# Attention's second stage: other places for biases, q and k, dense sums ahead of a step on DVE, and the last high and low parts in tiles of q and k

## The chip, the cores and the metric

The kernel runs on one core of one Trainium2 chip. A core has five engines that work beside each other, each through its own instructions in order: PE (TensorE, matmuls; the profile shows its weight loads apart, as PEld), DVE (VectorE), ACT (ScalarE), POOL (GpSimd) and SP (SyncE, which here only issues transfers). Matmuls read SBUF, the core's working memory, and write PSUM, 8 banks of 128 x 512 float32. DVE and ACT take the results from there. Transfers (DMAs) to and from DRAM are issued by SP and POOL.

The metric is the device time of one execution in microseconds (us). The profile is of one further execution, with its own time; its times are counted from the start of its span.

## What is computed

A trunk of two layers on x of 1024 tokens and 1024 features, each layer with a residual: first a gated short convolution, then dilated attention. Cut to the second layer, which the change touches:

```python
proj = rms_norm(x, attn_norm) @ w_in              # q, k, v of 3 groups, gate z
for g, (window, dilation) in enumerate(((128, 1), (512, 4), (2048, 16))):
    q, k = rms_norm(q_g, q_gain[g]), rms_norm(k_g, k_gain[g])
    logits = q @ k.T / 8 + bias_g                 # causal, banded, 16 heads of 64
    lse = logsumexp(logits)
    out_g = exp(logits - lse) @ v_g
alpha = softmax(stack(lse), axis=0)               # over the three groups
y = sum(alpha * out) * silu(z)
x = x + y @ w_out
```

All of it is float32. Large products are made of three matmuls on float32r parts: a value is split in a high part and a low part (value minus high), and high x high, high x low and low x high are added.

## The kernel before

**First stage, up to about 1649 us.** The convolution layer and the projections of q, k, v and z. Big products run as Strassen products of half size (`strassen`, `product`, L304 to L307): the right operands stand in SBUF blocks named a to g and xb, 16 KB per partition each, the weights pass through tiles `wr`, `ws` and `sr`. Normalized q and k, v and the gates go to DRAM (`qkd`, `vd`, `zd`). The last pair of products is of z. Its products read block e, then f, then, with those left over from the pair before, a, xb, d, b, g, and at the end a and b. The last value of z goes from PSUM through DVE (L316), POOL (L689) and ACT (L690, Silu) to DRAM.

**Second stage, from L812 on.** Attention on what was stored, and the output projection. All five engines run in an order written out by hand: the order in which the Python code issues instructions is the order on each engine. Heads go in 8 pairs, each with 3 groups, 24 units in all. `attention` returns for each unit 4 steps (groups 0 and 1) or 2 steps (group 2), 80 in all. A step has three parts:

- A (L887, L895, L898): PE makes the scores of q and k in two banks `ps` (a ring of 3), DVE adds the bias `bt` and takes the minimum, writing `xs`, ACT takes the exponential.
- B (L905, L843 or L845), 2 steps later (`LB`): PE transposes `xs` into `pt`, ACT or DVE copies it to `pts`.
- C (L918 or L924), 4 steps later (`LC`): PE multiplies with V into `po`; L935 copies it to `o`.

At the end of each head pair the weights of the three groups (L955 to L973) go through DRAM (`fd`) and come back spread over a tile `fb` (L981, issued by POOL). DVE scales the outputs with them (L984), POOL adds (L987), DVE multiplies with the gate (L990), and the result is split into a high part (L994, ACT) and a low part (L997, DVE) in a tile `y2`. For the last head pair there is no detour by DRAM: `wide`, `spread_last` and `last` (L1006 to L1032) do the same in halves, with tiles of the ring `qk` and PE transposes.

**The output projection** runs between the steps. The weights of a row come by `fetch` (L56), and `split` (L1075) and `split_low` (L1078) put their parts in tiles of the same ring `y2`, made by `parts_tile`, with 7 places for 16 tiles. From step 34 on, `some` issues for a step one partial sum over two head pairs (`dense`, L1064 to L1066, six matmuls) into a PSUM bank `pd`, of which there is one. `add_sums` (L1102, DVE) adds it to `acc`, in which the residual lies. There are 16 such sums for each of three rounds: steps 34 to 49, 54 to 69, and 74 to the end, where from step 80 on two come in a step, in other banks too. The fourth round, for the last two head pairs, stands at the end with its own adds (L1153) and the stores of the result.

**The loop that sets the order** goes over steps k. For each it issues, in this order of lags, A of step k, then `add_sums`, then what is due of earlier steps, C, and last B; then the dense matmuls of this step, then loads:

```python
for lag in (0, 1, LC, 3, *range(LC + 1, 15), LB):
    for f in steps[k - lag].get(lag, ()) if 0 <= k - lag < len(steps) else ():
        f()
    if lag == 0:
        add_sums()
for f in extra.get(k, ()):
    f()
```

**Memory.** Each pool's tiles get addresses in the order in which a tag is first used; pools opened later lie above. The pool `wp` (`y2`, `wraw`) lies lowest, where the first stage has its weight tiles, then `fbp` (`fb`), then `ap` (`acc`, `bt`, `qk`, `xs`, `V`, `pts`, `sz`, `o`). With `reuse_waits="tile"` a tile waits only for the last users of those earlier tiles whose memory it takes. SP's first issues of the stage are, in this order: two `bt` (L858) and two `qk` (L827) of the first unit, the same of the second, then V of the first (L835), then `bt` and `qk` of the third.

Of the kernel before, what the change touches and what calls it, by code (L numbers as in the profile page):

```python
# [10 lines left out]
F32 = mybir.dt.float32  # L11
F32R = mybir.dt.float32r
I32 = mybir.dt.int32
AF = mybir.ActivationFunctionType
OP = mybir.AluOpType
# [4 lines left out]
P = 128  # L20
D = 1024
S = 1024
KT = D // P
# [5 lines left out]
HP = H // 2  # L29
# [6 lines left out]
def trunk(ctx: ExitStack, tc: tile.TileContext, a, out):  # L36
    nc = tc.nc
# [16 lines left out]
    def raw_row(src):  # L54
        raw = wp.tile([P, 1024], F32, name="wraw", tag="wraw", bufs=2)
        nc.sync.dma_start(raw, src)  # L56
        return raw

    def parts_tile():

        t = wp.tile([P, 2, S], F32R, name="y2", tag="y2", bufs=7)
        return t

    def rsqrt(pool, src, n, name, y=None):
        if y is None:
# [64 lines left out]
    def half(hf):  # L130
        return slice(hf * HALF, hf * HALF + HALF)
# [8 lines left out]
    with tc.tile_pool(name="wq", bufs=1) as wq, tc.tile_pool(name="sle", bufs=1) as sle, \  # L140
# [197 lines left out]
        with tc.tile_pool(name="rp", bufs=1, side="right") as rp, tc.tile_pool(name="cp", bufs=2, side="right") as cp, \  # L338
# [31 lines left out]
            W = {}  # L370
# [443 lines left out]
    wp = ctx.enter_context(tc.tile_pool(name="wp", bufs=4, reuse_waits="tile"))  # L814
    with tc.tile_pool(name="sp", bufs=3, space=PSUM) as sp, tc.tile_pool(name="ptp", bufs=2, space=PSUM) as ptp, \
# [3 lines left out]
            tc.tile_pool(name="sm", bufs=2, reuse_waits="tile") as sm, \  # L819
            tc.manual_schedule(engines={getattr(mybir.EngineType, e)  # L820
                                        for e in ("PE", "DVE", "Activation", "Pool", "SP")}):
        QK, VS, SZ, y2, part = {}, {}, {}, {}, {}

        def loads(hp, g):
            QK[hp, g] = [ap.tile([P, S], F32, name="qk", tag="qk", bufs=6) for _ in range(2)]
            for i in range(2):
                nc.sync.dma_start(QK[hp, g][i], qkd[hp, g, i])  # L827
            if g == 2:
                SZ[hp] = ap.tile([P, S], F32, name="sz", tag="sz", bufs=2)
                nc.sync.dma_start(SZ[hp], zd[hp])  # L830
# [16 lines left out]
        def attention(hp, g):  # L847

            u = {}
            lo, up = slice(0, 64), slice(64, 128)  # L850
# [141 lines left out]
            def high():  # L992
                y2[hp] = parts_tile()
                nc.scalar.activation(y2[hp][:, 0], SZ[hp], AF.Copy)  # L994
# [24 lines left out]
            def last(hf, i):  # L1019
                h, z = half(hf), SZ[hp][:, half(hf)]  # L1020
                if i == 0:
                    for w in (2, 1, 0):
                        nc.vector.tensor_tensor(O[hp, w][:, h], O[hp, w][:, h], u["fb", w], op=OP.mult)  # L1023
                elif i == 1:
                    for w in (2, 0):
                        nc.vector.tensor_tensor(O[hp, 1][:, h], O[hp, 1][:, h], O[hp, w][:, h], op=OP.add)
                    nc.vector.tensor_tensor(z, O[hp, 1][:, h], z, op=OP.mult)
                    if hf == 0:
                        y2[hp] = parts_tile()
                    nc.scalar.activation(y2[hp][:, 0, h], z, AF.Copy)  # L1030
                else:
                    nc.vector.tensor_tensor(y2[hp][:, 1, h], z, y2[hp][:, 0, h].bitcast(F32), op=OP.subtract)  # L1032

            steps = []
            for q in range(2):
# [6 lines left out]
            if g == 2:  # L1042
                if hp == HP - 1:
                    todo = [(LB, weights), (3, shares), (3, wide), (LC, lambda: spread_last(0)),
                            (LC, lambda: last(0, 0)), (LC, lambda: last(0, 1))]
                    ending.update(spread=spread_last, last=last)
                else:
                    todo = [(3, weights), (LC, shares), (LC, store_shares), (LC, lambda: spread(2)),
                            (LC, lambda: spread(1)), (8, lambda: scale(2)), (8, lambda: spread(0)),
                            (9, lambda: scale(1)), (9, lambda: add(2)), (11, lambda: scale(0)),  # L1050
                            (11, lambda: add(0)), (12, gate), (13, high), (14, low)]
                for lag, f in todo:
                    end.setdefault(lag, []).append(f)
# [4 lines left out]
        W, ending = {}, {}  # L1058

        def dense(ps, kts, dt, hf, first, last):  # L1060
            ws, cs = slice(dt * P, dt * P + P), half(hf)
            for kt in kts:
                (whi, wlo), (hi, lo) = ((t[kt][:, 0], t[kt][:, 1]) for t in (W, y2))
                nc.tensor.matmul(ps, whi[:, ws], hi[:, cs], start=first and kt == kts[0], stop=False)  # L1064
                nc.tensor.matmul(ps, whi[:, ws], lo[:, cs], start=False, stop=False)  # L1065
                nc.tensor.matmul(ps, wlo[:, ws], hi[:, cs], start=False, stop=last and kt == kts[-1])  # L1066
# [6 lines left out]
        def split(kt):  # L1073
            W[kt] = parts_tile()
            nc.scalar.activation(W[kt][:, 0], raws[kt], AF.Copy)  # L1075

        def split_low(kt):
            nc.vector.tensor_tensor(W[kt][:, 1], raws[kt], W[kt][:, 0].bitcast(F32), op=OP.subtract)  # L1078

        acc = [ap.tile([P, S], F32, name="acc", tag=f"acc{dt}", bufs=1) for dt in range(KT)]  # L1080

        def residual(dt, hf):
            nc.sync.dma_start(acc[dt][:, half(hf)], x1d[dt, :, half(hf)])
# [9 lines left out]
        def some(kts, dt, hf, name):  # L1093

            ps = bank(name)
            dense(ps, kts, dt, hf, True, True)
            sums.append((ps, acc[dt][:, half(hf)]))

        def add_sums():
            while sums:  # L1100
                ps, x = sums.pop(0)
                nc.vector.tensor_tensor(x, ps, x, op=OP.add)  # L1102
# [18 lines left out]
        for r in range(3):  # L1121
            k0 = at[2 * r + 2, 0][0] + LD
            k = k0
            for i, (dt, hf) in enumerate(tiles):
                late = k >= len(steps)
                name = "pd" if not late else ("pd", ("ps", "ps", "pt", "pt")[min(k - len(steps), 3)])[i % 2]
# [9 lines left out]
            f()  # L1136
        k = 0
        while k < len(steps) + LC or any(x >= k for x in extra):
            for lag in (0, 1, LC, 3, *range(LC + 1, 15), LB):
                for f in steps[k - lag].get(lag, ()) if 0 <= k - lag < len(steps) else ():  # L1140
                    f()
                if lag == 0:
                    add_sums()
            for f in extra.get(k, ()):
                f()
            for f in begins.get(k, ()):
                f()
            k += 1
# [10 lines left out]
        for dt, hf, ps in first:  # L1159
            dense(ps, (6,), dt, hf, True, False)  # L1160
# [3 lines left out]
        for dt, hf, ps in first:  # L1164
            dense(ps, (7,), dt, hf, False, True)
# [77 lines left out]
```

## Time and profile before

| what | value |
|---|---|
| time, 3 runs | 2037.06, 2038.78, 2042.22 us; median 2038.78 |
| the profiled execution | 2040.09 us, span 2038.1 us |
| mean granted clock of TensorE | 0.988 |
| first and last score matmul (L887) | 1656.1 and 1978.0 us |
| first and last dense matmul into `pd` | 1772.8 and 2029.4 us |
| score reductions (L895) | 384, 291 ns median |
| sums (L1102) | 48, 685 ns median for those from `pd` |
| high parts of the last pair (L1030) | 2, at 2007.9 and 2017.9 us |

A row of the timeline reads: start in us, length, engine, line, operation, tile written <- tiles read, size, how many were merged; in brackets the idle time of that engine ahead of it and what ended that. A row of the waits reads: engine, what waited <- what it waited for: us in total, times, longest. A row by stretches has the stretch, its length, busy us and number of instructions of PE, PEld, DVE, ACT and POOL, the granted clock, the busy share of the DMA engines and GB/s.

### The profile page before, as it was taken

Reading aid. Unit: us, or ns where it says so; the run is one execution under the profiler, and the core shown is the slowest. Engines: PE = TensorE matmul, PEld = TensorE weight load, DVE = VectorE, ACT = ScalarE, POOL = GpSimd, SP = SyncE. Lnnn points to the kernel's source line nnn. Section 1 sums busy time; section 2 is a strip of 40 time slices with the busy share of each in tenths; the row PEclk is TensorE's granted clock in tenths of the full one; section 3 lists DMA queues with packets and bytes.
Section 4 is the critical chain, followed back from the end, with each engine's and each line's share of the span. In section 5 each row is a group of like instructions: output and inputs, shape, how many; then the busy total and the mean of one; then the engine's idle time right before and its main releaser. Section 6 shows DMA issues by size and latency. Waiting matters only on the chain. (4 is left out here: it accounts for less than half of the span.)

```text
span 2038.1 us, 29437 instructions
## 1 busy us (share of the span) xinstructions
PE 1958.5 (96%) x10302; PEld 1585.0 (78%) x10302; DVE 1481.0 (73%) x2751; ACT 903.5 (44%) x2042; POOL 879.8 (43%) x800
## 2 busy tenths in 40 slices
PE   7999999999999999999999999999999988898998
PEld 6887778888888888788888888888888866666666
DVE  6866566566666555798888888788888847767686
ACT  5433233333334344434344343444343358757570
POOL 0356566666665212434455445544445522322220
PEclk9999999999999999999999999999999999999999
DMA  5316512112214564423333233323233368766632
GB/s 189 114 62 146 141 61 73 68 67 73 72 64 152 178 228 159 131 76 111 102 105 123 84 111 97 123 83 121 86 124 104 91 241 248 219 175 207 181 115 84
DMA packets 116805, 254.25 MB, mean 125 GB/s; under 512 B 15822, under 2 KB 22718, under 8 KB 116656
## 3 DMA queue, kind: packets, MB, share of 16 engines
q1 hardware_dynamic: 93024, 177.42, 26.2%
q0 software_dynamic: 23632, 74.95, 12.9%
q8 instruction: 81, 1.33, 0.3%
q14 instruction: 68, 0.56, 0.1%
HBM read 193.05 MB, written 67.64 MB: 128 GB/s over the span
## 5 line engine op out<-in xcount | busy, mean ns | idle before, releaser
L170 DVE TENSOR_TENSOR ws<-wr,ws 128x512 fp32r<-128x512 f32 x284 | 270.2, 953 | 131.8 <-ACT ws L169 130.3
L169 ACT ACTIVATE ws<-wr 128x512 fp32r<-128x512 f32 x284 | 178.4, 630 | 395.6 <-PE pp L307 230.7
L169 ACT ACTIVATE ws<-sr 128x512 fp32r<-128x512 f32 x272 | 169.6, 629 | 295.9 <-PE pp L307 246.6
L279 POOL TENSOR_TENSOR sr<-wr 128x512 f32<-128x512 f32 x136 | 185.2, 1362 | 262.8 <-DMA wr<-in_conv_w_in 66.5
L170 DVE TENSOR_TENSOR ws<-sr,ws 128x512 fp32r<-128x512 f32 x272 | 235.6, 873 | 82.6 <-ACT ws L169 80.9
L898 ACT ACTIVATE xs<-xs,nl 128x128 f32<-128x128 f32 (+1 forms) x384 | 167.9, 439 | 91.2 <-DVE nl L895 80.2
L316 DVE TENSOR_TENSOR f<-pp,f 128x512 f32<-128x512 f32 x204 | 139.5, 684 | 85.5 <-PE pp L307 80.9
L895 DVE CUSTOM_DVE_ANT_0 xs<-ps,bt 128x128 f32<-128x128 f32 (+1 forms) x384 | 110.9, 347 | 79.5 <-PE ps L887 57.8
L312 ACT ACTIVATE f<-pp 128x512 f32<-128x512 f32 x228 | 132.5, 581 | 28.4 <-POOL blkc L683 13.4
L279 POOL TENSOR_TENSOR sr<-wr,sr 128x512 f32<-128x512 f32 x68 | 89.1, 1310 | 81.2 <-issue 57.6
L716 POOL DMA_DIRECT2D qkd<-blkc x96 | 68.1, 716 | 129.2 <-DVE blkc L711 121.8
L674 ACT ACTIVATE f<-f 128x512 f32<-128x512 f32 x96 | 60.7, 633 | 135.8 <-DVE f L316 98.8
L304 PE MATMUL pp<-blke,ws 128*128 128x512 f32 x272 | 108.7, 400 | 8.2 <-ACT f L312 8.2
L304 PE MATMUL pp<-blkg,ws 128*128 128x512 f32 x272 | 107.5, 395 | 4.8 <-ACT f L312 3.8
L306 PE MATMUL pp<-blkg,ws 128*128 128x512 f32 x272 | 106.7, 392 | 3.3 <-DVE blkg L524 3.3
L304 PE MATMUL pp<-blkf,ws 128*128 128x512 f32 x272 | 108.5, 399 | 0.7 <-ACT f L312 0.7
L304 PE MATMUL pp<-blka,ws 128*128 128x512 f32 x272 | 107.3, 395 | 0.7 <-ACT f L312 0.7
L306 PE MATMUL pp<-blke,ws 128*128 128x512 f32 x272 | 107.9, 397 | 0.0
L307 PE MATMUL pp<-blke,ws 128*128 128x512 f32 x272 | 107.8, 396 | 0.0
L304 PE MATMUL pp<-blkb,ws 128*128 128x512 f32 x272 | 107.4, 395 | 0.0
L304 PE MATMUL pp<-blkd,ws 128*128 128x512 f32 x272 | 107.0, 393 | 0.0
L887 PE MATMUL ps<-qk 64*128 64x128 f32 (+1 forms) x768 | 91.4, 355 | 15.7 <-DVE nl L895 8.6
(305 smaller groups left out, 5398.4 us busy)
## 6 DMA issues: line engine op xcount, KB each, us to landing
wr<-in_conv_w_in SPq DMA_DIRECT2D x128, 256.0 KB, 2.9
wr<-in_wqk SPq DMA_DIRECT2D x96, 256.0 KB, 3.0
qkd<-blkc POOLq DMA_DIRECT2D x96, 256.0 KB, 3.2
qk<-qkd SPq DMA_DIRECT2D x48, 512.0 KB, 7.1
wr<-in_conv_w_out SPq DMA_DIRECT2D x64, 256.0 KB, 3.2
f<-in_x SPq DMA_DIRECT2D x48, 256.0 KB, 4.5
wr<-in_wv SPq DMA_DIRECT2D x48, 256.0 KB, 2.9
vd<-f POOLq DMA_DIRECT2D x48, 256.0 KB, 2.4
```

The lines of the kernel that those rows point to most:

```text
L169: nc.scalar.activation(t[:, 0], src, AF.Copy)
L170: nc.vector.tensor_tensor(t[:, 1], src, t[:, 0].bitcast(F32), op=OP.subtract)
L279: nc.gpsimd.tensor_tensor(t, x, y, op=op)
L304: nc.tensor.matmul(ps, w[:, 0, ws], b[:, k, 0], start=new and k == 0, stop=False, skip_group_check=not new)
L306: nc.tensor.matmul(ps, w[:, 0, ws], b[:, k, 1], start=False, stop=False, skip_group_check=not new)
L307: nc.tensor.matmul(ps, w[:, 1, ws], b[:, k, 0], start=False, stop=end and k == 3, skip_group_check=not new)
L312: nc.scalar.activation(t, ps, AF.Copy)
L316: nc.vector.tensor_tensor(m, ps, m, op=OP.add)
L716: nc.gpsimd.dma_start(qkd[hp, g, which].rearrange("p (c s) -> p c s", c=c) [:, :, hf * m:(hf + 1) * m], o.rearrange("p (c s) -> p c s", c=c))
L887: nc.tensor.matmul(out_, q[hs, b * P:(b + 1) * P], k[hs, kv], start=True, stop=True)
L895: nc.vector.tensor_tensor_reduce(out=x, in0=ps[s][:, x0:x0 + nk].rearrange("p a b -> p (a b)"), in1=u["bt"][s][:, bs], op0=OP.add, op1=OP. ...
L898: nc.scalar.activation(x, x, AF.Exp, bias=nm, scale=-1.0, accum_out=L)
```

## The change

`parts_tile` moves into the second stage and takes its tiles from the pool `ap`. The tag `y2` is then first used after all others of that pool, so its 56 KB lie above them and no longer below `fb`, `acc`, `bt` and `qk`. The line of `acc` moves up within the stage; it is the pool's first tile as before. The last head pair's high and low parts are two tiles of the ring `qk` in place of one `y2` tile, and `dense` picks them by the head pair. `add_sums` is called at the head of a step, ahead of A.

```diff
-    def parts_tile():
-
-        t = wp.tile([P, 2, S], F32R, name="y2", tag="y2", bufs=7)
-        return t
...
+        def parts_tile():
+
+            t = ap.tile([P, 2, S], F32R, name="y2", tag="y2", bufs=7)
+            return t
+
         QK, VS, SZ, y2, part = {}, {}, {}, {}, {}
+        acc = [ap.tile([P, S], F32, name="acc", tag=f"acc{dt}", bufs=1) for dt in range(KT)]
...
                     if hf == 0:
-                        y2[hp] = parts_tile()
-                    nc.scalar.activation(y2[hp][:, 0, h], z, AF.Copy)
+                        y2[hp] = [ap.tile([P, S], F32R, name="qk", tag="qk", bufs=6) for _ in range(2)]
+                    nc.scalar.activation(y2[hp][0][:, h], z, AF.Copy)
                 else:
-                    nc.vector.tensor_tensor(y2[hp][:, 1, h], z, y2[hp][:, 0, h].bitcast(F32), op=OP.subtract)
+                    nc.vector.tensor_tensor(y2[hp][1][:, h], z, y2[hp][0][:, h].bitcast(F32), op=OP.subtract)
...
-                (whi, wlo), (hi, lo) = ((t[kt][:, 0], t[kt][:, 1]) for t in (W, y2))
+                whi, wlo = W[kt][:, 0], W[kt][:, 1]
+                hi, lo = y2[kt] if kt == HP - 1 else (y2[kt][:, 0], y2[kt][:, 1])
...
-        acc = [ap.tile([P, S], F32, name="acc", tag=f"acc{dt}", bufs=1) for dt in range(KT)]
...
         while k < len(steps) + LC or any(x >= k for x in extra):
+            add_sums()
             for lag in (0, 1, LC, 3, *range(LC + 1, 15), LB):
                 for f in steps[k - lag].get(lag, ()) if 0 <= k - lag < len(steps) else ():
                     f()
-                if lag == 0:
-                    add_sums()
```

## The prediction, made before the changed kernel was run

> **What bounds the kernel now.** The first view is the page's busy times, the second the busy times of each engine by stretches of the run.
>
> ```profile
> PE 1958.5 (96%) x10302; PEld 1585.0 (78%) x10302; DVE 1481.0 (73%) x2751; ACT 903.5 (44%) x2042; POOL 879.8 (43%) x800
> ...
> 1600.00:1649.00 49.00, 47.89 (x218) 38.95 (x216) 31.30 (x48) 14.89 (x26) 27.48 (x30) 1.00 0.37 113
> 1649.00:1656.00 7.00, 0.00 (x0) 0.00 (x0) 0.67 (x1) 1.91 (x2) 1.83 (x2) 0.80 0.88 280
> 1656.00:1772.00 116.00, 103.49 (x1081) 79.09 (x1081) 82.96 (x393) 96.84 (x375) 26.40 (x30) 0.92 0.81 254
> 1772.00:1990.00 218.00, 197.66 (x1804) 147.04 (x1805) 158.56 (x614) 143.12 (x535) 58.54 (x65) 1.00 0.58 170
> ```
>
> TensorE bounds the whole run. Everything before 1649 is untouched by the change. From there the columns (PE, PEld, DVE, ACT, POOL, clock, DMA) show two losses: 7.00 us with no matmul at all between the stages, and a stretch of 218.00 us, the one with the output projection's matmuls among the attention's, in which PE works 197.66 and no other engine is full. The waits name what ends them (engine waiting, line, releaser: us, times, longest):
>
> ```profile
> PE ps L887 <- DMA qk<-qkd: 7.1, 1, 7.1
> ...
> PEld pd L1064 <- DVE acc L1102: 25.6, 30, 1.2
> PE pd L1064 <- DVE acc L1102: 18.4, 26, 1.0
> ```
>
> The last two rows are of 1770 to 1990 and the same waits seen twice. I take PEld's 25.6: a weight load starts the group, and the matmul's modelled end reaches some 0.25 us into the idle time that PE's own row counts.
>
> **Part 1, tiles moved in memory.** In the order of first use, the pools lie from the end of the constants upwards. The first stage has there, by its tile sizes: wr 0 to 8 KB, ws to 40, sr to 46, block f 46 to 62, e 62 to 78, a 78 to 94, b 94 to 110, g to 126, d to 142, c to 158. Now y2 (7 x 8 KB) comes first, then wraw to 64, fb to 72, acc to 104, bt 104 to 110, q and k 110 to 134: bt lies on block b, the last block that a matmul reads. Without y2 in that pool, everything slides down by 56 KB: bt 48 to 54 on f, q and k 54 to 78 on f and e, V from 90 on a and b. acc is the first tile of its pool in both kernels, so moving its line does nothing. The change of stage, in order of time (start, length, engine, line, out<-in, idle time and releaser):
>
> ```profile
> 1626.54 0.39 PE L307 MATMUL pp<-blkf,ws 128*128 128x512 f32 x1
> ...
> 1645.83 0.39 PE L307 MATMUL pp<-blka,ws 128*128 128x512 f32 x1
> ...
> 1648.55 0.39 PE L307 MATMUL pp<-blkb,ws 128*128 128x512 f32 x1
> 1648.97 0.83 SPq L858 DMA_DIRECT2D bt<-sk  x2
> 1648.98 0.69 DVE L316 TENSOR_TENSOR f<-pp,f 128x512 f32<-128x512 f32 x1 [2.03 <-PE pp L307]
> 1649.75 1.26 POOL L689 TENSOR_TENSOR f<-f,sqacc 128x512 f32<-128x512 f32 x1 [1.30 <-DVE f L316]
> 1649.90 0.85 SPq L827 DMA_DIRECT2D qk<-qkd  x2
> 1651.04 0.63 ACT L690 ACTIVATE f<-f 128x512 f32<-128x512 f32 x1 [3.43 <-POOL f L689]
> 1651.69 1.28 ACT L898 ACT_TABLE_LOAD   x1
> 1656.08 4.31 PE L887 MATMUL ps<-qk 64*128 64x128 f32 x18 [7.15 <-DMA qk<-qkd]
> 1658.18 0.40 ACT L898 ACTIVATE xs<-xs,nl 128x128 f32<-128x128 f32 x1 [5.21 <-DVE nl L895]
> ```
>
> SP issues bt 0.03 us after the last matmul on b ends (1648.55 + 0.39); behind it wait q and k. Blocks e and f are read for the last time at 1626.54 + 0.39 = 1626.9, so the four bt and four q/k loads of the first two units can leave 22 us earlier, and 6.2 us (1649.90 to 1656.08) bring the first of them in. PE's first matmul of the stage then has its data at 1649. SP's next load, V, waits for block a until 1646.2; behind it stand bt, q, k and z of the third unit, which left at 1654 and later before, so nothing on SP becomes later. Those early loads run beside weights that are already in, in a stretch with a DMA share of 0.37: they cost nothing.
>
> What is late next is ACT, not PE. The last gate value goes DVE L316, POOL L689, ACT L690, and only then does ACT load its table, up to 1651.69 + 1.28 = 1652.97. None of these four depends on the moved tiles. Before, the first exponential started at 1658.18. From there ACT is the stage's first bound (96.84 of 116.00 us above, and nearly without a gap at first). So the gain is 1658.18 - 1652.97 = **5.2 us**, not the 7.15 of the wait. Bounds: 0 if the loads stay where they are; 10.3 if PE sets the start, since then 18 matmuls also take 1.2 us (16 take 1.16 at full clock, in the row of 1743.73 below) in place of 4.31.
>
> **Part 2, dense sums first.** A step on PE is: scores (L887), values (L924), transposes (L905), dense (L1064 to L1066) into the one bank pd. DVE's step is four to eight score reductions (L895) and only then the sum (L1102) that frees pd. Two steps, one without and one with the wait:
>
> ```profile
> 1774.43 0.71 PE L887 MATMUL ps<-qk 64*128 64x128 f32 x8
> ...
> 1778.53 1.13 PE L887 MATMUL ps<-qk 64*128 64x256 f32 x8
> ...
> 1783.19 0.40 PE L1066 MATMUL pd<-y,y 128*128 128x512 f32 x1
> 1783.51 1.14 PE L887 MATMUL ps<-qk 64*128 64x256 f32 x8
> 1784.79 0.43 DVE L895 CUSTOM_DVE_ANT_0 xs<-ps,bt 128x256 f32<-128x256 f32 x1 [2.59 <-PE ps L887]
> 1786.17 0.68 DVE L1102 TENSOR_TENSOR acc<-pd,acc 128x512 f32<-128x512 f32 x1
> 1786.91 0.19 PEld L1064 LDWEIGHTS pd<-y,y 128*128 128x128 f32 x1 [0.88 <-DVE acc L1102]
> 1788.50 0.72 PE L887 MATMUL ps<-qk 64*128 64x128 f32 x8
> ```
>
> The first step takes 1778.53 - 1774.43 = 4.10 us, the second 1788.50 - 1783.51 = 4.99; the difference is the wait of 0.88. The sum's operand is complete at 1783.19 + 0.40 = 1783.6, and DVE sits idle for 2.59 us until 1784.79 for the scores. Put at the head, the sum runs there, 1783.6 to 1784.3: it ends before the reductions can start, delays nothing on DVE or ACT, and frees pd at 1784.3, when PE wants it at 1786.91 - 0.88 = 1786.0. It adds no instruction and no new wait, for the scores come later on PE than the dense sums that it waits for. So the 25.6 us go, except where DVE is late itself:
>
> ```profile
> 1819.24 1.22 DVE L997 TENSOR_TENSOR y<-sz,y 128x1024 fp32r<-128x1024 f32 x1
> ...
> 1821.95 0.19 PEld L1064 LDWEIGHTS pd<-y,y 128*128 128x128 f32 x1 [0.93 <-DVE acc L1102]
> ```
>
> Here DVE is free at 1820.46, the sum would end at 1821.1, PE wants the bank at 1821.0: 0.1 to 0.5 stays, at three such places 1 us. Shorter steps leave DVE 158.56 and ACT 143.12 us in some 192: no bound. I take off 0.5 more for single waits behind them: **24.1 us**. Bounds: 12 if half of the waits return in another place, 26.8 with 0.6 us more at the two places where stretches without dense work, bound by DVE, begin one sum earlier.
>
> **Part 3, the last high and low parts in q/k tiles.** They no longer wait for a y2 tile that the dense matmuls still read:
>
> ```profile
> ACT y L1030 <- PE pt L1066: 12.0, 1, 12.0
> ...
> 2012.56 1.71 PE L1016 MATMUL ps<-ident,qk 64*128 64x64 f32 x24
> 2013.30 1.88 DVE L1023 TENSOR_TENSOR o<-o,ps 128x512 f32<-128x512 f32 x3 [3.79 <-PE ps L1016]
> 2015.10 0.68 DVE L1032 TENSOR_TENSOR y<-sz,y 128x512 fp32r<-128x512 f32 x1
> 2015.84 0.51 PE L1065 MATMUL pt<-y,y 128*128 128x512 f32 x1 [1.15 <-DVE y L1032]
> ```
>
> ACT's 12.0 us vanish, but nobody waits for it: L1032 stands on DVE behind three multiplications that PE's transposes release at 2013.30, and PE's 1.15 us hang on that. The tiles (4th and 5th of the ring of six behind the three that L1006 and L1008 fill) were last read by score matmuls some 20 us earlier. Worth 0; its cover is that DVE order. In the last steps no scores are left, so the moved sums stand where they stood.
>
> **The sum.** 5.2 + 24.1 + 0 = 29.3 us. The profiled execution took 2040.09 us (span 2038.1 and 2.0 around it), so it becomes 2010.8; against the median of 2038.78 that is **2009.5 us**.
>
> **Rivals.** (a) The scale factors come late. They go by DRAM (store, then four loads of fb), and their time does not shrink with the steps:
>
> ```profile
> 1710.77 1.22 DVE L984 TENSOR_TENSOR o<-o,fb 128x1024 f32<-128x1024 f32 x1 [3.96 <-DMA fb<-fd]
> 1712.89 2.07 PE L887 MATMUL ps<-qk 64*128 64x128 f32 x14 [3.56 <-DVE nl L895]
> ...
> 1743.73 1.16 PE L887 MATMUL ps<-qk 64*128 64x128 f32 x16
> ...
> 1776.28 2.09 POOL L981 DMA_DIRECT2D fb<-fd  x4 [2.54 <-DMA fd<-fo]
> 1787.37 1.22 DVE L984 TENSOR_TENSOR o<-o,fb 128x1024 f32<-128x1024 f32 x1
> fb<-fd POOLq DMA_DIRECT2D x4, 256.0 KB, 9.8
> ```
>
> L984 needs the first two of the four, which leave at 1776.28 and 1776.80 and at 9.8 us, the median of the four, land by 1786.6. It starts at 1787.37, and would come up two removed waits of 0.88 and one sum of 0.68 earlier, at 1784.9. So a wait of up to 1.7 us is possible; at 2 us in each of five head pairs that is 10 us, and 2019.5. (b) **The slower side** is the same mechanism as it stands at 1710: a wait of 3.96 us on DVE holds back the scores, PE stands for 3.56 and then runs 14 matmuls in 2.07 where 16 take 1.16 (about 3 us until it is back at full pace). At 6.5 us in five head pairs that is 33 against the 29.3 won: 2042. It decides from some 3.5 us of lateness on; for it speaks that the stretch up to 1772 has it twice, against it that the stretch from 1772 has no row of it and a DMA share of 0.58, not 0.81. (c) The loads do not move, because something else holds SP: gain 24.1, 2014.7. Against it: SP's rows show nothing of its own between the last weight and bt. (d) PE, not ACT, sets the start: 10.3 + 24.1, 2004.4. The profile's row gives the price of a cold start, 18 matmuls in 4.31 us after 7.15 of idleness. [...]
>
> **How the numbers follow.** Forecast (2006 to 2013): 0.65. (a) 0.15, (c) 0.06, (d) 0.08, (b) 0.03, no change because both waits turn into others 0.03. A measurement here tells changes above 0.3% (6 us) from none. Only (b) ends slower, only the last within 6 us: faster 0.94, same 0.03, slower 0.03. The range runs from (d) with the upper bound of part 2 (10.3 + 26.8 = 37.1, so 2002) to (a) at 2020.
>
> **What would show it.** Part 1: bt issued near 1627, PE's pause at 1649 gone, the first exponential close to 1653; if the table load comes later, the 5.2 shrink. Part 2: the row PEld pd from DVE acc falls from 25.6 to about 1, steps of 4.1 us; if waits of pd remain with DVE busy, or fb appears among the releasers of L984 after 1770, (a) is at work. Part 3: L1030 waits no more, and PE's 1.15 us at the end stay. A pause of PE above 3 us anywhere after 1656 would make the forecast wrong.

## The result, and the profile after

| | before | after |
|---|---|---|
| time, 4 runs | 2037.06 to 2042.22, median 2038.15 us | 2009.19 to 2014.02, median 2011.91 us |
| ratio of the runs | | 0.9866, 95% interval 0.9849 to 0.9883 |
| profiled execution | 2040.09 us, span 2038.1 | 2009.19 us, span 2007.3 |

26.2 us are gained by the medians; 29.3 were forecast. A second measurement of the unedited changed kernel (the last experiment but one) gave 0.9894, interval 0.9877 to 0.9910, or 22.6 us between the medians. Both belong to the result: by the medians the kernel is faster by 22 to 26 us. A profile shows one execution, which need not lie at the median: of the four after it was the quickest (2009.19).

In the kernel after, the first stage's lines have numbers 5 lower (L304 is L299), those of the second stage up to L1032 one higher (L984 is L985), and L1064 to L1066 are L1066 to L1068. PE is the bound as before, by the page's busy times:

```profile
PE 1948.4 (97%) x10302; PEld 1583.3 (79%) x10302; DVE 1482.8 (74%) x2751; ACT 903.7 (45%) x2042; POOL 881.5 (44%) x800
```

**Where the time came from.** The first stage, which the change doesn't touch, ends (last matmul on block b) at 1648.94 us in the one profile and at 1642.46 in the other. Over all the profiles of this study that point lies anywhere between 1642.46 and 1649.00, so these 6.5 us say nothing of the change, and I count from there. The second stage falls into three stretches: A up to the first dense matmul, B from there to the last row of score matmuls, C to the end of the span. Busy times by stretch, before (stretch, length, busy us and instructions of PE, PEld, DVE, ACT, POOL, clock, DMA share, GB/s):

```profile
1648.94:1772.87 123.93, 104.36 (x1088) 79.90 (x1089) 84.45 (x397) 99.17 (x377) 28.23 (x32) 0.92 0.80 253
1772.87:1977.13 204.26, 184.78 (x1697) 136.54 (x1695) 149.19 (x586) 136.82 (x513) 53.69 (x63) 1.00 0.62 181
1977.13:2038.10 60.97, 52.75 (x355) 41.78 (x354) 38.52 (x79) 9.40 (x27) 4.85 (x3) 0.97 0.19 70
```

And after:

```profile
1642.46:1765.22 122.76, 105.08 (x1089) 80.54 (x1089) 84.80 (x397) 99.36 (x377) 28.45 (x33) 0.92 0.76 233
1765.22:1946.64 181.42, 177.46 (x1697) 135.83 (x1695) 149.44 (x585) 134.40 (x505) 53.27 (x62) 1.00 0.72 204
1946.64:2007.30 60.66, 52.52 (x355) 41.76 (x354) 39.76 (x80) 11.27 (x35) 5.28 (x3) 0.97 0.19 71
```

The stage is 24.3 us shorter (389.16 to 364.84): 1.2 in A, 22.8 in B, 0.3 in C. So the sums delivered, and of the 5.2 us of part 1 only 1.2 are left by the end of A (2.2 in the second profile of the same kernel). Yet they were won. The timeline after, at the change of stage:

```profile
1621.38 0.85 SPq L828 DMA_DIRECT2D qk<-qkd  x2
...
1642.39 1.35 PE L888 MATMUL ps<-qk 64*128 64x128 f32 x10
...
1645.22 1.28 ACT L899 ACT_TABLE_LOAD   x1
...
1646.52 0.40 ACT L899 ACTIVATE xs<-xs,nl 128x128 f32<-128x128 f32 x1
```

q and k are issued 21 us before the stage starts, PE goes over to the scores without a pause, and the first exponential comes 1646.52 - 1642.46 = 4.06 us after the start, where it was 1658.18 - 1648.94 = 9.24: 5.2 us. Then this happens (timeline after, DVE, PE and POOL):

```profile
1700.47 1.23 DVE L985 TENSOR_TENSOR o<-o,fb 128x1024 f32<-128x1024 f32 x1 [4.60 <-DMA fb<-fd]
1702.59 2.07 PE L888 MATMUL ps<-qk 64*128 64x128 f32 x14 [4.21 <-DVE nl L896]
...
1752.13 0.57 POOL L942 DMA_DIRECT2D ml<-nld  x1 [6.89 <-DVE nl L896]
...
1755.12 1.22 DVE L991 TENSOR_TENSOR sz<-o,sz 128x1024 f32<-128x1024 f32 x1 [2.59 <-POOL o L988]
...
1758.22 1.61 PE L888 MATMUL ps<-qk 64*128 64x256 f32 x6 [2.99 <-DVE nl L896]
```

The scale factors are late; DVE waits for them with the scores queued behind, and PE stands. Then POOL holds its load of `ml` ahead of an addition, the gate waits for the addition, and PE stands again. The load waits for the stores that it reads to land: the last of them was issued at 1741.2 and took 10.4 us, to 1751.6, though the row names DVE. PE's own waits in A add up like this, before (two rows) and after:

```profile
PE ps L887 <- DVE nl L895: 8.6, 5, 3.6
PE ps L887 <- DMA qk<-qkd: 7.1, 1, 7.1
...
PE ps L888 <- DVE nl L896: 12.3, 6, 4.2
PE pt L906 <- ACT pts L846: 4.6, 6, 2.2
```

The 7.1 us for q and k are gone; the waits for reductions on DVE have grown by 3.7 us, and those for ACT's copies by 1.3 (they were 3.3). Waits for fb add up to 17.2 us in 10 places (9.6 in 5 before), 12.1 of them up to 1770 and 5.1 behind, by the views of the waits:

```profile
DVE o L985 <- DMA fb<-fd: 17.2, 10, 4.6
...
PEld pd L1066 <- DVE acc L1102: 2.8, 1, 2.8
```

The second row is part 2: of the weight loads' waits for the bank, one is left, near the end of the span, and it was there before. Dense steps now look like this (timeline, PE and DVE):

```profile
1808.89 0.72 PE L888 MATMUL ps<-qk 64*128 64x128 f32 x8
1809.00 0.69 DVE L1102 TENSOR_TENSOR acc<-pd,acc 128x512 f32<-128x512 f32 x1 [0.43 <-PE pd L1068]
1812.97 1.14 PE L888 MATMUL ps<-qk 64*128 64x256 f32 x8
1813.08 0.69 DVE L1102 TENSOR_TENSOR acc<-pd,acc 128x512 f32<-128x512 f32 x1 [1.71 <-PE pd L1068]
1817.04 1.14 PE L888 MATMUL ps<-qk 64*128 64x256 f32 x8
```

The sum runs 0.1 us behind the start of the next scores, in DVE's idle time, and a step takes 4.07 to 4.08 us where one with the wait took 4.99.

### The profile page after: what moved, and what is told of

The parts are those of the page before. It is cut to its first block, busy times and chain, and to the rows that moved or that the text cites. A ratio compares the mean times of both kernels' runs of the same rounds, so it can differ in the third digit from the quotient of the medians.

```text
span 2007.3 us, 29480 instructions
## 1 busy us (share of the span) xinstructions
PE 1948.4 (97%) x10302; PEld 1583.3 (79%) x10302; DVE 1482.8 (74%) x2751; ACT 903.7 (45%) x2042; POOL 881.5 (44%) x800
## 4 chain that ended last, share of the span: by engine, by line
PE 66%; DVE 10%; issue 5%; DMA 2%; ACT 2%; POOL 1%; DVEq 0%; POOLq 0%; ACTq 0%; SPq 0%
PE pp L299 16%; PE pp L301 15%; PE pp L302 15%; PE pp L550 3%; PE pp L551 3%; PE pp L549 3%; PE ps L888 2%; DVE ws L165 2%; PE pt L906 2%; PE po L925 2%; DVE blkc L706 1%; DVE ri L67 1%; DMA nld<-nl 1%; ACT xs L899 1%; DVE st L670 1%
## 5 line engine op out<-in xcount | busy, mean ns | idle before, releaser
L165 DVE TENSOR_TENSOR ws<-wr,ws 128x512 fp32r<-128x512 f32 x284 | 268.4, 947 | 126.8 <-ACT ws L164 125.4
L307 ACT ACTIVATE f<-pp 128x512 f32<-128x512 f32 x228 | 132.5, 581 | 26.8 <-POOL blkc L678 12.9
L669 ACT ACTIVATE f<-f 128x512 f32<-128x512 f32 x96 | 60.7, 633 | 139.0 <-DVE f L311 101.8
L299 PE MATMUL pp<-blke,ws 128*128 128x512 f32 x272 | 108.2, 398 | 6.8 <-ACT f L307 6.8
L299 PE MATMUL pp<-blkg,ws 128*128 128x512 f32 x272 | 107.6, 396 | 4.6 <-ACT f L307 3.7
L301 PE MATMUL pp<-blkg,ws 128*128 128x512 f32 x272 | 106.8, 393 | 3.3 <-DVE blkg L519 3.3
L299 PE MATMUL pp<-blkf,ws 128*128 128x512 f32 x272 | 108.6, 399 | 0.7 <-ACT f L307 0.7
L299 PE MATMUL pp<-blka,ws 128*128 128x512 f32 x272 | 107.2, 394 | 0.7 <-ACT f L307 0.7
L299 PE MATMUL pp<-blkb,ws 128*128 128x512 f32 x272 | 107.5, 395 | 0.0
L299 PE MATMUL pp<-blkd,ws 128*128 128x512 f32 x272 | 107.0, 394 | 0.0
L302 PE MATMUL pp<-blkg,ws 128*128 128x512 f32 x272 | 106.5, 391 | 0.0
```

What stands on the lines that cost most here:

```text
L165: nc.vector.tensor_tensor(t[:, 1], src, t[:, 0].bitcast(F32), op=OP.subtract)
L299: nc.tensor.matmul(ps, w[:, 0, ws], b[:, k, 0], start=new and k == 0, stop=False, skip_group_check=not new)
L301: nc.tensor.matmul(ps, w[:, 0, ws], b[:, k, 1], start=False, stop=False, skip_group_check=not new)
L302: nc.tensor.matmul(ps, w[:, 1, ws], b[:, k, 0], start=False, stop=end and k == 3, skip_group_check=not new)
L307: nc.scalar.activation(t, ps, AF.Copy)
L669: nc.scalar.activation(sq, t, AF.Square)
```

## The experiments

Theory: the sums carry the gain (some 22 us, all in B); part 1's 5.2 us are real but are taken back in A by waits of fixed place, namely for the scale factors and behind POOL's load of `ml`; part 3 is worth 0. Rivals: the gains add up and what is missing is scatter; or the trips of the factors have a length of their own.

The table has each kernel's ratio to the kernel before on the same chip, from all its runs, and from its one profiled execution the first exponential (in us from the stage's start) and the lengths of the three stretches and of the stage.

| kernel | ratio (95% interval) | first exp. | A | B | C | stage |
|---|---|---|---|---|---|---|
| before | | 9.24 | 123.9 | 204.3 | 61.0 | 389.2 |
| after | 0.9866 (0.9849 to 0.9883) | 4.06 | 122.8 | 181.4 | 60.7 | 364.8 |
| after, again | 0.9894 (0.9877 to 0.9910) | 4.05 | 121.7 | 183.8 | 62.4 | 367.9 |
| e1_memory | 0.9987 (0.9975 to 0.9999) | 4.05 | 127.6 | 204.6 | 61.0 | 393.1 |
| e2_sums | 0.9895 (0.9876 to 0.9914) | 10.05 | 129.8 | 182.4 | 59.1 | 371.3 |
| e3_tiles | 1.0006 (0.9993 to 1.0019) | 9.18 | 125.4 | 204.3 | 59.3 | 388.9 |
| e7_mem_resid | 0.9968 (0.9955 to 0.9981) | 4.05 | 119.3 | 204.5 | 62.3 | 386.1 |
| e6_ml | 0.9837 (0.9816 to 0.9858) | 4.06 | 124.3 | 178.1 | 59.2 | 361.6 |
| e8_resid | 0.9857 (0.9843 to 0.9870) | 4.05 | 118.5 | 180.7 | 62.4 | 361.6 |
| e5_late | 0.9861 (0.9844 to 0.9877) | 4.05 | 125.0 | 179.4 | 60.0 | 364.4 |
| e11_late_nl | 0.9850 (0.9827 to 0.9873) | 4.06 | 122.3 | 179.4 | 59.9 | 361.6 |
| e9_all | 0.9856 (0.9840 to 0.9872) | 4.05 | 117.8 | 181.9 | 58.5 | 358.2 |
| e10_nl | 0.9820 (0.9805 to 0.9835) | 4.05 | 114.9 | 180.9 | 58.4 | 354.2 |
| e14_no_part1 | 0.9863 (0.9844 to 0.9881) | 9.52 | 122.2 | 185.5 | 60.1 | 367.8 |

C lies between 58.4 and 62.4 with no order by edit. It goes by PE's clock: near the end of the span PE stands for 2.34 us for a sum in every one of the 14 profiles. In the six in which its clock stayed full behind that pause (1.00 over all of C in e10_nl) C is 58.4 to 59.9, in the eight in which it fell to half (0.50 from 1973.8 to 1976.0 in the kernel after) 60.0 to 62.4.

### The three parts alone

**e1_memory**: the kernel before with the hunks of `parts_tile` and `acc`.

> The kernel before with part 1 alone: the ring y2 is taken from the pool of the attention's tiles, the line of acc moves up; the sums stay behind the scores, the last parts stay in a y2 tile. Theory A (part 1 wins 5.2 us at the start of the stage and the trips of the scale factors and POOL's load of ml, whose times are fixed, take nearly all of it back before step 34): the first exponential comes about 4 us after the last matmul on block b ends (9.2 before), the lead at the first dense matmul is 0 to 2 us, and the kernel is 0 to 2.5 us faster, 2036 to 2038. Theory B (what is won at the start is kept, and the 5 us that the forecast was too hopeful by are scatter or belong to the sums): 5.2 us faster, 2033.

The interval of the ratio reaches from 0.2 to 5.1 us; the medians differ by 1.9 us. The lead is 4.4 us some 45 us into the stage, and then it is lost with more. Timeline of e1_memory, POOL, DVE and PE:

```profile
1698.61 1.59 POOL L982 DMA_DIRECT2D fb<-fd  x3 [8.60 <-DMA fd<-fo]
...
1708.85 1.23 DVE L985 TENSOR_TENSOR o<-o,fb 128x1024 f32<-128x1024 f32 x1 [10.61 <-DMA fb<-fd]
...
1710.97 2.07 PE L888 MATMUL ps<-qk 64*128 64x128 f32 x14 [10.21 <-DVE nl L896]
```

The first pair's trip (from the end of the last L974 to the first L985) took 20.0 us here; it was 13.3 before, 14.0 after, 16.8 in e2_sums and 12.5 in e3_tiles. The number is theory A's, and the interval just leaves out theory B's 5.2 us. Theory A's reason holds in part: the lead goes where it said, in DVE's wait for the factors, but the trip is no fixed length; it is the most variable thing in the stage. How much of the lead one execution keeps therefore differs: with the residual's loads beside the trip, A is 123.9, 125.4 and 129.8 us in the three kernels without part 1, and 121.7 to 127.6 in the profiles of e1_memory, e6_ml and the changed kernel.

**e2_sums**: the kernel before with the hunk of the loop.

> The kernel before with part 2 alone: the sums stand at the head of a step on DVE, the memory and the last parts stay. Theory A (the sums carry nearly the whole gain): 24 to 26 us faster, 2012 to 2014, the waits of a weight load for the bank pd fall from 25.6 us to 3 or less, and the pause of 7.15 us at the start of the stage stays. Theory B (the gains of the parts add, and part 1 has 5.2 of the 26.2): 20 to 22 us faster, 2016 to 2018.

By the medians 20.2 us (the ratio says 17.5 to 25.3): nearer to theory B's number than to theory A's, though the interval holds both. The stretches decide: B is 182.4, like 181.4 and 183.8 with all parts, where kernels with the sums behind the scores have 204.3 to 204.6. So the sums are worth 20.4 to 22.8 us in B, less than theory A said, and B owes nothing to part 1. What e2_sums lacks lies in A, 129.8 us: its start was slow (24 scores in 6.37 us after a pause of 7.96), and the trip of pair 0 made DVE wait for 7.40 us.

**e3_tiles**: the kernel before with the hunks of `last` and `dense`.

> The kernel before with part 3 alone: the last head pair's high and low parts are two tiles of the ring of q and k. Theory (ACT's 12.0 us wait is covered by DVE's order, in which the scaling of the second half stands ahead of the low part): 0, within 1 us, 2037 to 2039; ACT's wait for the matmuls that read the y2 tile is gone, and PE's wait for the low part at the end stays at 1.1 to 1.2 us. Rival (the earlier high part draws the low part and the last matmuls forward): up to 1.2 us faster at the end of the span, PE's wait there gone.

No difference that the time could tell. The waits decide against the rival: PE's pause at the end stays. In the kernel after, it and ACT's wait read:

```profile
1985.07 0.50 PE L1067 MATMUL pt<-qk,y 128*128 128x512 f32 x1 [1.15 <-DVE qk L1033]
1987.11 0.64 ACT L1031 ACTIVATE qk<-sz 128x512 fp32r<-128x512 f32 x1 [14.77 <-DVE sz L1028]
```

ACT now waits for DVE's product (21.3 us in two waits) where part of it was for PE (12.0), and the 1.15 us on PE are what they were.

### What takes part 1's lead

**e7_mem_resid**: e1_memory with the residual's loads later. In e1_memory the DMA engines had a busy share of 0.88 (268 GB/s) from 1689 to 1709, the 20 us of pair 0's trip, and SP's loads of the residual lie in that time, which makes them a suspect for a trip that POOL issues.

```diff
-            when(4 + i, residual, dt, hf)
+            when(28 + i, residual, dt, hf)
```

> The kernel of e1_memory (part 1 alone), with the sixteen loads of the residual (256 KB each) issued at steps 28 to 43, not 4 to 19; they are first needed at steps 35 to 50. Theory A1 (the trip of the first head pair's factors is long, 13.3 to 20.0 us in the runs where later pairs take 13.2 to 17.1 without a wait, because other transfers fill the engines of the DMA): the wait of 10.61 us before the first multiplication of pair 0 falls below 3, part 1's lead of 4.4 us lives until step 23, and the kernel is 4 to 8 us faster than before, 2032 to 2036. Theory A2 (the trip's time is its own, whatever else is moved): as e1_memory, 0.9987 of before, 2036 to 2038.

8.1 us by the medians, 6.5 by the ratio. Pair 0's trip took 10.8 us and its first wait 1.44 in place of 10.61; A is 8.3 us shorter than in e1_memory, whose trip was the longest of all, and 4.6 shorter than before; B is the same. A1 holds: with the loads that SP issues moved away, the trip that POOL issues is 9.2 us shorter, at a DMA share of 0.68 (222 GB/s, 1693 to 1704), not 0.88. Over all the profiles, pair 0's trip took 10.5 to 12.0 us in the five with the residual's loads moved and 12.5 to 20.0 in the nine with them beside it. The kernel before with the residual alone moved was not run, so e7_mem_resid doesn't tell the lead that is kept from what the loads cost any kernel; e14_no_part1 below does. **e8_resid** is the same edit to the changed kernel.

> The changed kernel with the sixteen loads of the residual at steps 28 to 43, not 4 to 19. Theory A1 (other transfers make the factors' trip long): pair 0's trip falls from 14.0 us (16.0 and 16.8 in two other runs with the same loads) to 13 or less and its wait from 4.60 below 3; pair 1, with none of these loads beside it in either kernel, keeps its 4.29 to within 1; 2 to 5 us faster than the changed kernel, 2007 to 2010. The dense stretch gets 256 KB more in each step: should the sums wait there for acc or the factors of pair 2 for their trip, the gain is gone, 2012 to 2015. Theory A2 (the trip's time is its own): 2011 to 2013.

Trip 10.5 us, wait 1.15, pair 1's wait 3.80, all as A1 has it; A is 118.5, 3 to 4 us less than in the two profiles without the edit. The loads of pair 0's factors in e1_memory, the extreme case, then in the changed kernel (line, engine, count: length in ns, first and last issue; then issue to landing):

```profile
L982 POOL DMA_DIRECT2D fb<-fd x4: 515/532/550, 1698.6 to 1700.2; - x4
...
DMA to landing us min/median/max: 8.7/10.1/12.1
...
L982 POOL DMA_DIRECT2D fb<-fd x4: 515/531/550, 1694.1 to 1695.7; - x4
...
DMA to landing us min/median/max: 4.6/6.4/7.6
```

and the same four in e8_resid:

```profile
L982 POOL DMA_DIRECT2D fb<-fd x4: 517/532/552, 1697.6 to 1699.2; - x4
...
DMA to landing us min/median/max: 3.5/4.4/5.2
```

The same 4 x 256 KB land at a median of 4.4 us without the residual's 256 KB a step beside them, where the changed kernel has 6.4. The residual doesn't account for every long landing: pair 1's four, which have none of it beside them, took 6.9 to 11.9 us in e8_resid too. The time, 2010.53 us, lies between the two forecasts, and 0.9857 can't be told from the changed kernel's 0.9866.

**e6_ml**: the changed kernel, POOL's load of `ml` behind the additions.

```diff
-            for lag in (0, 1, LC, 3, *range(LC + 1, 15), LB):
+            for lag in (0, LC, 3, *range(LC + 1, 15), 1, LB):
```

> The changed kernel, but with what is due one step after a unit's end (the stores of nl and the load of ml, on POOL) issued behind the additions and spreads of the same step, not ahead of them. The load of ml waits 6.89 us on POOL at 1745 to 1752 in the changed kernel, and the last addition of the head pair before stands behind it, then the gate (2.59 us on DVE), then the scores (a pause of 2.99 us on PE). Theory A (this wait is one of those that take back part 1's lead): the gate's wait and PE's pause near 1758 are gone, 2 to 5 us faster than the changed kernel, 2007 to 2010. Rival (another wait, the scale factors', ends as late): DVE's next wait for fb grows by as much and the time stays at 2011 to 2013. Theory B (the rest is scatter): the same 2011 to 2013, with the waits gone and nothing in their place.

The time came out at 2006.31 us, a little better than forecast; the interval of its ratio lies below that of the changed kernel's second measurement but overlaps the first's. The gate no longer waits, and something small stands in its place: DVE now waits for `ml` (timeline of e6_ml).

```profile
1758.88 1.22 DVE L991 TENSOR_TENSOR sz<-o,sz 128x1024 f32<-128x1024 f32 x1
...
1765.41 0.17 DVE L956 TENSOR_TENSOR mx<-ml 128x16 f32<-128x16 f32 x1 [2.80 <-DMA ml<-nld]
```

The gain isn't in A (124.3, with a trip of 16.0 us in this run) but in B: 178.1, the shortest of all. There PE works 176.4 us and stands for 1.7, where it stands for 4.0 in the changed kernel; the gate's waits for POOL, 0.4 to 0.6 us in each of four head pairs there, are gone, and DVE's waits for fb behind 1770 fall from 5.1 to 1.0 us.

**e5_late**: the changed kernel, a free tile of the first stage for the third factor, and two multiplications a step later.

```diff
-                fb = u["fb", w] = fbp.tile([P, S], F32, name="fb", tag="fb")
+                fb = u["fb", w] = fbp.tile([P, S], F32, name="fb", tag="fb") if w else sqacc
...
-                            (LC, lambda: spread(1)), (8, lambda: scale(2)), (8, lambda: spread(0)),
-                            (9, lambda: scale(1)), (9, lambda: add(2)), (11, lambda: scale(0)),
+                            (LC, lambda: spread(1)), (LC, lambda: spread(0)), (9, lambda: scale(2)),
+                            (10, lambda: scale(1)), (10, lambda: add(2)), (11, lambda: scale(0)),
```

> The changed kernel, with the spread of the third scale factor issued with the other two (its tile is one of the first stage's, which is free), and the first two multiplications with the factors one step later (9 and 10 steps after the unit's end, not 8 and 9). Theory A (late factors hold the score reductions back on DVE, and that takes back what part 1 won): DVE's waits for fb, 17.2 us in 10 in the changed kernel, fall below 4 us, as a step is 3.6 to 4.1 us long and the waits ahead of the first multiplication are 4.60 and 4.29; the pauses of 4.21 and 3.88 us on PE before step 34 go, and the time is 5 to 8 us below the changed kernel, 2004 to 2007. Rival (six transfers at once: the first two land later by what the third adds, some 3 us): the waits stay, 2010 to 2013.

A miss: the waits for fb fell from 17.2 to 6.6 us, not below 4, and the time stayed at 2010.94. A new wait took their place (timeline, DVE and PE):

```profile
1716.01 0.29 DVE L896 CUSTOM_DVE_ANT_0 xs<-ps,bt 128x128 f32<-128x128 f32 x1 [5.35 <-DMA acc<-x1d]
1716.71 1.64 PE L888 MATMUL ps<-qk 64*128 64x256 f32 x6 [4.26 <-DVE nl L896]
```

A score reduction reads no `acc`; the releaser named is only the transfer that landed about then. What the reduction also does is write `nl`, a ring of three, and the tile's last reader is the store to `nld`. That store, by tile:

```profile
L944 POOL DMA_DIRECT2D nld<-nl x1: 924/924/924, 1701.1 to 1701.1; - x1
...
DMA to landing us min/median/max: 14.7/14.7/14.7
```

1701.1 + 14.7 = 1715.8: DVE goes on 0.2 us later. In the changed kernel the same store landed 8.4 us after its issue; here POOL issues the third factor's two transfers ahead of it. **e11_late_nl** tests that: e5_late with `bufs=6` for `nl`.

> The kernel of e5_late with six places for the tiles nl (128 B per partition each), not three. Theory A (in e5_late the third factor's two transfers stand on POOL's queue ahead of the store of nl, which then lands 14.7 us after its issue, 8.4 in the changed kernel; the scores three units later write into the same place and wait 5.35 and 5.21 us on DVE for that): both waits are gone, with PE's pauses of 4.26 and 4.24 us behind them; the second stage comes from 364.42 to 355 to 359 us, and the time to 2001 to 2006. Rival (the wait is for the biases or for q and k, as the profile names other transfers too): the waits stay at 4 to 5.5 us, the stage at 363 to 365 us, and the time at 2009 to 2013.

The store lands as late as before (15.0 us at the least for the three of that step), and the reduction no longer waits: that it waited for its place in the ring `nl` is shown. That the two transfers ahead are what makes the store late is argued from the order alone. The size was missed, for now the third factor itself is late (timeline, DVE):

```profile
1719.82 1.23 DVE L985 TENSOR_TENSOR o<-o,sqacc 128x1024 f32<-128x1024 f32 x1 [3.48 <-DMA sqacc<-fd]
```

### All of them, and part 1 undone again

**e9_all** has the edits of e5_late, e6_ml and e8_resid.

> The changed kernel with the edits of e5_late, e6_ml and e8_resid together: third factor's spread with the other two and the first two multiplications a step later, POOL's stores and load one step after a unit's end behind the additions, residual at steps 28 to 43. If each takes away a wait of its own, the second stage, 364.84 us in the changed kernel and 361.65 with POOL's order alone, comes to 354 to 358 us, and the time to 2000 to 2005. If they all shorten one and the same chain, it is no shorter than the best of them alone, 2004 to 2007.

358.2 us in the stage, just above what was expected, but 2010.21 in the time, 5 us more than that (the profiled execution took 2004.19, the least of the four); it has the wait for `nl` too (5.45 us, at 1745.65). **e10_nl** is e9_all with `bufs=6` for `nl`.

> The kernel of e9_all with six places for the tiles nl. Theory A as in e11_late_nl: the wait of 5.45 us at the start of head pair 2 and that of 2.49 us a pair later are gone, and the second stage comes from 358.25 us to 350 to 353, the time to 1997 to 2004. Rival (waits for biases or q and k): 357 to 359 us, 2004 to 2010.

2001.63 us, 0.9820, the lowest median of the study: its interval lies below both of the changed kernel's, and overlaps e6_ml's. The wait is gone; the stage, 354.2, is 1 us longer than forecast. Its three stretches, by busy times:

```profile
1645.28:1760.17 114.89, 101.92 (x1089) 77.50 (x1089) 85.50 (x398) 98.99 (x377) 28.88 (x33) 0.94 0.76 222
1760.17:1941.09 180.92, 177.45 (x1698) 135.81 (x1696) 150.92 (x584) 135.52 (x509) 51.86 (x61) 1.00 0.81 221
1941.09:1999.50 58.41, 50.94 (x355) 40.59 (x354) 41.71 (x80) 10.51 (x31) 5.26 (x3) 1.00 0.20 73
```

A is 7 to 8 us shorter than in the two profiles of the changed kernel. **e12_again** is the changed kernel, unedited.

> The changed kernel once more, with nothing edited, to see how far its second stage differs from one profiled execution to the next: 364.84 us the first time. If the length of the first head pair's trip (12.5 to 20.0 us in runs with the residual's loads beside it) is chance, the stage may come out anywhere from 363 to 371 us; the time is 0.985 to 0.988 of the kernel before, 2009 to 2014.

Pair 0's trip was 13.4 us this time; the stage is 3.1 us longer than in the first profile (A 1.1 shorter, B 2.4 and C 1.7 longer). B's 2.4 us have one cause, seen on PE (timeline; the second row is by stretches):

```profile
1842.82 2.07 PE L888 MATMUL ps<-qk 64*128 64x256 f32 x6 [1.73 <-DVE nl L896]
...
1842.82:1849.60 6.78, 6.78 (x54) 5.50 (x54) 6.61 (x27) 6.39 (x21) 0.00 (x0) 0.50 0.00 1
```

The gate waited 1.74 us for POOL, PE stood for 1.73, and then ran at half clock for 6.8 us: in B it works 180.05 us for the same matmuls, not 177.46. The time, 2016.51, is above what I expected. So 3 us in the stage or 0.3% in the time tell little between two kernels here; e5_late, e8_resid, e9_all and e11_late_nl are not told from the changed kernel by their times, nor e6_ml from its first measurement, and their verdicts rest on the waits.

**e14_no_part1** is e10_nl with the ring y2 in the lowest pool again.

```diff
-            t = ap.tile([P, 2, S], F32R, name="y2", tag="y2", bufs=7)
+            t = wp.tile([P, 2, S], F32R, name="y2", tag="y2", bufs=7)
```

> The kernel of e10_nl with part 1 undone: the ring y2 in the pool that lies lowest, as before the change, so the first biases, q and k wait for block b again and the first exponential comes about 9.2 us after the stage's start, not 4.05. Theory A (the lead won at the start lives on where the waits for the factors, POOL's load and nl are gone): the second stage comes from 354.22 to 358.5 to 361 us, that is 4.3 to 6 us longer, and so does the time, 2005 to 2009. Rival (the lead is taken back anyway, since the transfers of the first head pairs set the pace): 353 to 356 us, 2000 to 2004.

```profile
1653.30 6.64 PE L888 MATMUL ps<-qk 64*128 64x128 f32 x24 [7.42 <-DMA qk<-qkd]
```

That row of its timeline is the pause of the kernel before, with a slow run of scores behind it. The stage is 13.6 us longer, the medians differ by 12.2 and the ratios by 0.43%, or 8.8 us: more than the 4.3 to 6 forecast. A has 7.3 of it, which is the start: 9.52 - 4.05 = 5.5, and the rest from the slow scores, since e10_nl's lead over it is 8.0 us some 25 us into the stage. Pair 0's trip can't be the reason: 11.7 us here and 12.0 in e10_nl. In B, 4.6 us longer, a wait of 2.63 for q and k shows on PE, with half clock for 3.4 us behind it (16 multiplications with V in 1.98 us, where 1.09 is usual); whether it comes from the memory or from scatter stays open, and C's 1.7 go with the clock at the end, as above. The rival falls: with the other waits cleared, A keeps what part 1 wins at the start.

## Why the prediction was right

The forecast, 2009.5 us, lies 2.4 below the first median and 7.0 below the second; as a ratio, 2009.5 / 2038.78 = 0.9856, it stands inside the first interval and a little below the second. The direction and the main term were right. That the number came so near is partly luck: of the 29.3 us that were added up, the stage shows 24.3 in one profile and 21.3 in the other, and what the first median has beyond that is within the scatter of the first stage.

- **Part 2** (24.1, bounds 12 to 26.8) measured 22.8 and 20.4 us in B in the two profiles, and 21.8 in e2_sums. The mechanism is as told: the 25.6 us of waits for the bank are gone altogether, also at the three places where some was to stay. The term is 1 to 4 us too large, and the 0.5 us that I took off for waits behind is what was too small. In the first profile PE stands 2.2 us in B for reductions and a copy on DVE, where late factors (5.1 us in 5 waits) and the gate behind POOL's load stand ahead of them; in e6_ml, with most of both gone, none of the 2.2 is left. In the second profile one such pause took the clock as well, which cost 2.6 us more.
- **Part 1** (5.2) was right at its place, on the row named for it: the table load ends, the first exponential follows, 5.2 us earlier. The step that failed is that this gain was carried to the end of the run. I looked for what would be late next at the start, and named ACT; I did not look for what is late next 54 us further on (1646.52 to 1700.47 in the profile after). The row of 1710.77, DVE waiting 3.96 us for fb, was in the prediction, but as a price for the shorter steps of part 2, not as the place where part 1's lead would go. e1_memory shows it going there; e14_no_part1 beside e10_nl shows it staying, 7.3 us in A, where the trip is short and the other waits are cleared; e7_mem_resid and e8_resid agree.
- **Part 3** (0) is right, and for the reason given: DVE's order covers it. ACT's 12.0 us didn't vanish, though; they became a wait for DVE.
- **Rival (a)**, late factors, is the one partly at work. Its place was wrong: 2 us in each of five head pairs from 1770 on were feared, and there they are 5.1 us of waits on DVE, of which PE felt at most the 2.2 named above; the price lies up to 1770. **(b)** didn't come in the first profile, and once in the second, after a pause of 1.73 us, not of 3.5. That it decides from some 3.5 us on was an estimate from the row of 1712.89, and no run shows such a limit: in the kernel before, half clock (0.50 from 1749.4 to 1755.4) goes with a pause of 2.48 us too. Behind the pause in that row, of 3.56, the clock stood at 0.50 for 5.1 us, up to 1718.0; the 3 us named there are what of it lies behind the 14 scores. Its 2042 is 3 us above the median before, within the 6 that were said to tell nothing, so its chance belonged with no change. **(c)** didn't come, nor **(d)**: ACT set the start. (By the row cited for it, 18 matmuls take 1.3 us, not 1.2; its 10.3 is 0.1 too large.)
- **The mark for a wrong forecast**, a pause of PE above 3 us after 1656, was badly chosen. There were two, of 4.21 and 3.88 us; but the kernel before has 3.56 and 2.48 at the same places. A mark has to be a difference to what stands there already.
- **PE's clock** didn't stay full through the start, though the 5.2 us stand: it fell only behind the first exponential. The first ten scores follow without a pause and at full clock (1.35 us; 1.00 from 1642.0 to 1643.7), but further on PE stood for 2.22 us, and the clock did fall (after, timeline and by stretches):

```profile
1652.74 0.99 PE L906 MATMUL pt<-ident,xs 128*128 128x128 f32 x4 [2.22 <-ACT pts L846]
...
1653.00:1656.00 3.00, 3.00 (x24) 2.41 (x22) 0.93 (x8) 3.00 (x13) 0.91 (x1) 0.50 0.98 342
```

The traces show no length of pause from which the clock falls: pauses of 2.22 us here and 1.73 in the second profile were enough, and at the start of e12_again and of e10_nl eight scores took 2.08 us, where the row of 1812.97 above has 1.14, with no pause above 0.41 before them. And of the pause of 2.34 us that all 14 profiles have near the end of the span, 8 saw the clock fall to half within the 3 us behind it and 6 did not. Where the half clock falls differs too. Timeline rows of L888 in e1_memory and in e8_resid, the same 14 scores after the same pause, each with PE's clock by stretches:

```profile
1747.11 1.16 PE L888 MATMUL ps<-qk 64*128 64x128 f32 x14 [3.40 <-DVE nl L896]
...
1748.29:1755.10 6.81, 5.90 (x38) 4.52 (x40) 5.31 (x27) 6.08 (x28) 3.17 (x3) 0.50 1.04 302
```

```profile
1741.27 2.07 PE L888 MATMUL ps<-qk 64*128 64x128 f32 x14 [3.40 <-DVE nl L896]
...
1740.30:1747.00 6.70, 5.73 (x36) 4.83 (x38) 5.88 (x36) 5.75 (x28) 4.94 (x5) 0.50 1.06 336
```

Both lost the clock for some 6.8 us; in e1_memory it fell only behind the scores. So the next row alone doesn't show whether a pause cost clock.

## What to carry to other kernels

A lead won early is kept only if nothing between there and the end waits for something that didn't move: walk the waits of the whole stage, and ask of each whether it would simply grow by the lead. The same trip through DRAM took from 10.5 to 20.0 us here; before one is counted on, see which loads run beside it and which of them could go later. And when one wait is taken out, read which tile's ring, or which instruction queued behind it, becomes the next, for the profile may name another transfer as releaser.

## What the runs showed of the hardware

- Pair 0's four 256 KB loads of the factors landed at a median of 5.3 to 10.1 us in the nine profiles with the residual's loads beside them and of 4.4 to 5.0 in the five without; the 24 KB store ahead of them after 6.2 to 8.9 against 4.9 to 6.0 us.
- A 16 KB store landed 8.4 us after its issue in the changed kernel, and 14.7 in e5_late, where POOL issues two more 256 KB loads ahead of it; over all profiles the same store took 6.3 to 12.2 us without those two ahead and 9.6 to 16.2 with them.
- The same pause of PE, 2.34 us, was followed by half clock (0.50 in the kernel after) in 8 of 14 profiles and by full clock in 6; once 1.73 us was enough (0.50 for 6.8 us, e12_again).
- The same instructions in the same order ended the first stage anywhere within 6.5 us from one execution to the next.
